# A gate's softplus written with |z| on ScalarE in a hybrid attention and convolution step

## The chip, the cores and the metric

The kernel runs on one core of one Trainium2 chip. The metric is device microseconds (us) of one execution. Beside the times there is one profiled execution, taken by the hardware profiler; its rows are the source of every duration below. The engines are PE (TensorE matmul; PEld its weight loads), DVE (VectorE), ACT (ScalarE), POOL (GpSimd) and SP (SyncE, which issues all DMAs here). The programs are built with a scheduler that fixes each engine's instruction order before the run; on the chip each engine then follows its own list in order and waits on semaphores.

## The reference, cut to what matters

One layer. A normalised input (2048 prompt rows, 16 meta rows, 32 sample rows, 1024 wide) goes through one projection of 4096 columns. Four attention heads and four convolution units of 128 columns each follow, each with a gate z·sigmoid(z) (SiLU); then an output projection, a residual add and a norm.

```
q, k, v, z_a, b_g, c_g, u, z_c = split_proj(rmsnorm(hp, norm_g[l]), w_in[l])
...
o = rmsnorm(o, sub_g) * (1.0 - lam_init)
o = o.reshape(*o.shape[:2], W_ATT) * jax.nn.silu(z_a)
y_c = jax.nn.silu(z_c) * b_g * conv_out
return jnp.concatenate([o, y_c], axis=-1) @ w_o
```

The kernel gets sigmoid(z) as exp(-softplus(-z)), softplus(-z) = log(1 + exp(-z)), since exp and log serve everywhere else in it.

## The kernel before, in words

The prompt is cut into four passes p = 0..3 of 512 rows; pass 0 also carries the 48 meta and sample rows and is projected in two blocks of 272 to 288 columns, the others in one block of 512. In each pass `unit_a(h, p)` projects q, k, v and the gate z of head h, `attend(h, p)` does its two softmaxes and the product with v, and `unit_c(u, p)` does a convolution unit with its own gate. Each projection (`proj`, L225) is 24 matmuls of three split products: weights and inputs are cut into a high and a low part (`wh`, `wl`, `xh`, `xl`), the high ones cast by ACT (L204, L152), the low ones subtracted on POOL or DVE (L78, L153). A projection ends in PSUM (`pj`, two buffers) and is evicted on DVE: q at L254, k at L280, v at L305, z at L352 and L572. The evicted v is transposed by PE (L316), so PE waits there for L305.

Attention scores `s` (L446, L447; three PSUM buffers) are reduced on DVE (L396, or L393 for the last stretch with the bias) and turned to exponentials by ACT (L397), which frees the buffer. `coefs` (L370 to L377) merges the stretches' sums, L400 and L401 scale and combine the two softmaxes, PE transposes the result (L462), ACT and DVE split it (L465, L466) and L469 to L471 multiply it with v.

`softplus_neg(out, z)` (L186 to L191) runs in `ev_z` (L353) and in `ev_g` (L573), once for each block of columns: 40 calls, 24 of them 512 wide (p = 1 to 3) and 16 of them 272 wide (p = 0). `unit_c` follows it with an exponential (L574) and two products; attention keeps it as `l1` until `post`, where L427 adds it to the logarithm of the norm and L428 takes one exponential of the sum.

Ahead of each later pass, `x_stats(p)` squares eight tiles on ACT (L115), reduces them on DVE (L117), `x_rms(p)` builds a diagonal matrix on DVE (L127), multiplies it on PE (L129) and copies it out on ACT (L130); `x_load(p)` splits the new inputs (L152, L153). At the end `out_first` and `out_rest` do the output projection (L693, L685): `load_cat` reads a tile `ct` and splits it (L671, L78), `half_product` adds the residual (L694) and the sum of squares (L695), L727 to L731 scale the rows, and SP stores them (`out<-y`).

Of the kernel before, what the change touches and what calls it, by code (L numbers as in the profile page):

```python
# [13 lines left out]
AF = mybir.ActivationFunctionType  # L14
ALU = mybir.AluOpType
# [32 lines left out]
def hybrid_step(ctx: ExitStack, tc: tile.TileContext, x, xT, ckT, cv, scT, rel_bias, norm_g, w_in,  # L48
# [20 lines left out]
    V, S, G, T = nc.vector, nc.scalar, nc.gpsimd, nc.tensor  # L69
# [3 lines left out]
    def halved(out, a, b, op, engine=None):  # L73

        n = out.shape[-1] if len(out.shape) == 2 else out.shape[1]
        cuts = (0, n // 2, n) if engine is None and n * (out.shape[-1] if len(out.shape) > 2 else 1) > 256 else (0, n)
        for c0, c1 in zip(cuts, cuts[1:]):
            (engine or G).tensor_tensor(out[:, c0:c1], a[:, c0:c1], b[:, c0:c1], op=op)  # L78
# [106 lines left out]

    def softplus_neg(out, z):  # L186

        V.tensor_scalar(out, z, -1.0, 40.0, op0=ALU.mult, op1=ALU.min)
        S.activation(out, out, AF.Exp)
        S.activation(out, out, AF.Ln, bias=1.0)  # L190
        V.scalar_tensor_tensor(out, z, -1.0, out, op0=ALU.mult, op1=ALU.max)  # L191


    pre = {}
# [14 lines left out]
    def proj(col, p, evac):  # L209
        w2 = pre.pop((col, p), None) or w_load(col, p)  # L210
        if p > 0:
            blks = [(0, QT)]
        elif col < CK or CZ <= col < CC or col >= CG:
            blks = [(NM, 288), (288, 560)]
        else:
            blks = [(0, 280), (280, 560)]
        for b0, b1 in blks:
            if p == 0 and col == CV:
                ps = ps_s.tile([P, 512], F32, tag="s", name="pj")[:, :b1 - b0]
            else:  # L220
                ps = ps_j.tile([P, 512], F32, tag="pj", name="pj")[:, :b1 - b0]
            for k in range(KT):
                wh, wl = w2[k // 4]
                for i, (a, b) in enumerate(((wh, xh), (wh, xl), (wl, xh))):
                    T.matmul(ps, lhsT=a[:, k % 4], rhs=b[k][:, b0:b1],  # L225
                             start=(k == 0 and i == 0), stop=(k == KT - 1 and i == 2))
            evac(ps, b0, b1)
# [9 lines left out]
    def unit_a(h, p):  # L237
# [113 lines left out]
        def ev_z(ps, b0, b1):  # L351
            V.tensor_tensor(z32[:, b0:b1], ps, rbs[p][:, b0:b1], op=ALU.mult)  # L352
            softplus_neg(l1[:, b0:b1], z32[:, b0:b1])  # L353
# [63 lines left out]
    def post(n, o32, sq, z, l1, dst):  # L417
        sqh, sql = (ap.tile([P, 2, 256], F32R, tag=t_, name="sqh").rearrange("p a b -> p (a b)")[:, :n]
                    for t_ in ("ah", "al"))
        V.tensor_copy(sqh, sq)  # L420
        V.tensor_tensor(sql, sq, f32(sqh), op=ALU.subtract)
        ps = ps_o.tile([P, 512], F32, tag="po", name="pss")[:, :n]
        T.matmul(ps, lhsT=ones_r, rhs=sqh, start=True, stop=False)
        T.matmul(ps, lhsT=ones_r, rhs=sql, start=False, stop=True)
        f = o_tile(n)
        S.activation(f, ps, AF.Ln, scale=1.0 / P, bias=leps[:, 0:1])
        V.scalar_tensor_tensor(f, f, 0.5, l1, op0=ALU.mult, op1=ALU.add)  # L427
        S.activation(f, f, AF.Exp, scale=-1.0)  # L428
        V.scalar_tensor_tensor(o32, o32, g2[:, 0:1], f, op0=ALU.mult, op1=ALU.mult)
        halved(o32, o32, z, ALU.mult)  # L430
        dma(dst, by_tile(o32) if n == QT else o32)

    def attend(h, p, st):
# [5 lines left out]
        for b in range(2):  # L439
# [40 lines left out]
            S.copy(o32[:, 256 * b:256 * (b + 1)], po)  # L480
            S.activation(sq[:, 256 * b:256 * (b + 1)], po, AF.Square)
        post(QT, o32, sq, z32[:, f0:f0 + QT], l1[:, f0:f0 + QT], cat[p][:, :, h])

    def attend_sample(h, st):
# [37 lines left out]
        V.tensor_tensor(o32[0], o32[0], o32[1], op=ALU.add)  # L522
        S.activation(sq, o32[0], AF.Square)
        post(NS, o32[0], sq, z32[:, NM + QT:], l1[:, NM + QT:], cat_s[:, h])


    def unit_c(u, p):
        tw = NX + QT if p == 0 else QT
        bn = tw + 4 if p == 0 else tw + 2
        ch = g_tile(bn)  # L530
        f0 = NM if p == 0 else 0
        hn = f0 + QT
        V.tensor_copy(ch[:, 0:2], hist[:, u])
        if p == 0:
            V.tensor_copy(ch[:, 2 + hn:4 + hn], scs[:, u])
        c32 = g_tile(tw)

        def ev_c(ps, b0, b1):
            V.tensor_tensor(c32[:, b0:b1], ps, rbs[p][:, b0:b1], op=ALU.mult)
            halved(c32[:, b0:b1], c32[:, b0:b1], rbs[p][:, b0:b1], ALU.mult)  # L540
        proj(CC + u, p, ev_c)

        def spans(b0, b1):
            return [(b0, min(b1, hn), 2)] + ([(hn, b1, 4)] if b1 > hn else [])

        def ev_u(ps, b0, b1):
            for s0, s1, off in spans(b0, b1):
                V.tensor_tensor(ch[:, s0 + off:s1 + off], ps[:, s0 - b0:s1 - b0], c32[:, s0:s1], op=ALU.mult)
        proj(CU + u, p, ev_u)
        V.tensor_copy(hist[:, u], ch[:, hn:hn + 2])  # L550
        if p == 0:
            dma(cT_s[P * u:P * (u + 1)], ch[:, bn - 2:])
        if p == NQ - 1:
            dma(cT_p[P * u:P * (u + 1)], ch[:, bn - 2:])
        yc = g_tile(bn - 2)
        V.tensor_scalar(yc, ch[:, :bn - 2], cw[:, 0, u:u + 1], None, op0=ALU.mult)
        V.scalar_tensor_tensor(yc, ch[:, 1:bn - 1], cw[:, 1, u:u + 1], yc, op0=ALU.mult, op1=ALU.add)
        V.scalar_tensor_tensor(yc, ch[:, 2:], cw[:, 2, u:u + 1], yc, op0=ALU.mult, op1=ALU.add)

        t4 = g_tile(tw)  # L560
        for s0, s1, off in spans(f0, tw):
            halved(yc[:, s0 + off - 2:s1 + off - 2], yc[:, s0 + off - 2:s1 + off - 2], rbs[p][:, s0:s1], ALU.mult)

        def ev_b(ps, b0, b1):
            for s0, s1, off in spans(b0, b1):
                V.tensor_tensor(t4[:, s0:s1], ps[:, s0 - b0:s1 - b0], yc[:, s0 + off - 2:s1 + off - 2], op=ALU.mult)
        proj(CB + u, p, ev_b)
        e, zc = g_tile(tw), g_tile(tw)

        def ev_g(ps, b0, b1):  # L570
            eb = e[:, b0:b1]
            V.tensor_tensor(zc[:, b0:b1], ps, rbs[p][:, b0:b1], op=ALU.mult)  # L572
            softplus_neg(eb, zc[:, b0:b1])  # L573
            S.activation(eb, eb, AF.Exp, scale=-1.0)  # L574
            halved(zc[:, b0:b1], zc[:, b0:b1], t4[:, b0:b1], ALU.mult)
        proj(CG + u, p, ev_g)
        V.tensor_tensor(t4[:, f0:], zc[:, f0:], e[:, f0:], op=ALU.mult)
        dma(cat[p][:, :, 4 + u], by_tile(t4[:, f0:hn]))
        if p == 0:
            dma(cat_s[:, 4 + u], t4[:, hn:])  # L580
# [232 lines left out]
```

## Time and profile before

| what | value |
| --- | --- |
| time, median of 3 runs | 1292.07 us (1292.02 to 1293.26) |
| profiled execution, own time | 1293.26 us |
| its span, first to last instruction | 1291.5 us |
| busy: PE / DVE / ACT / POOL | 1267.5 / 923.9 / 827.5 / 699.0 us |
| mean granted TensorE clock | 0.995 |
| DMA moved | 198.74 MB, mean 154 GB/s |

Busy time is the time in which at least one instruction of the engine runs; matmuls overlap each other, so PE's busy time is not a sum of single durations. The view by stages cuts the span into stretches and gives each engine's busy time in each. The view of waits says which instruction's end ended an idle time. In the timeline a row is start, duration, engine, line, operation, and what is written from what; a bracket gives idle time before the row and what ended it. ACT instructions that stand back to back overlap by a little, so what one costs in a full queue is the distance between starts.

### The profile page before, as it was taken

The page shows a single profiled execution, that of the slowest core. Times are in us where ns is not written, and L with a number is a line of the kernel's source. Part 1 is how long each engine was busy: PE and PEld are TensorE (multiplying, and loading weights), DVE is VectorE, ACT ScalarE, POOL GpSimd, SP SyncE. Part 2 cuts the span into 40 slices and gives each one's busy share as a digit, 9 for nine tenths or more (in the row PEclk, how much of TensorE's full clock was granted, in tenths as well). Part 3 has the DMA queues.
Part 4 walks back from the last instruction along what each step waited for, and adds up shares of the span by engine and source line. Part 5 has one row for each costly group of instructions (what it writes and reads, how often), then busy time and mean ns, then how long its engine had stood idle before and what let it go on. Part 6 is the DMA issues. An engine that isn't in the chain of part 4 may idle for free.

```text
span 1291.5 us, 21630 instructions
## 1 busy us (share of the span) xinstructions
PE 1267.5 (98%) x7058; PEld 1101.4 (85%) x7058; DVE 923.9 (72%) x2086; ACT 827.5 (64%) x2030; POOL 699.0 (54%) x918
## 2 busy tenths in 40 slices
PE   8999999999999998999999999999999999999897
PEld 6999999988888886888888888888888888888675
DVE  8767566567886847787878677767786896856654
ACT  6745454675776647677767567777777786763322
POOL 5775857767565675455556555364656483432200
PEclk9999999999999999999999999999999999999999
DMA  9834444774445347444343453344334543557652
GB/s 290 226 116 129 141 112 116 216 241 149 137 117 159 125 145 228 156 137 134 101 169 124 142 177 114 116 147 119 117 109 141 177 133 124 177 181 237 215 181 81
DMA packets 108048, 198.74 MB, mean 154 GB/s; under 512 B 17408, under 2 KB 45600, under 8 KB 107936
## 3 DMA queue, kind: packets, MB, share of 16 engines
q1 hardware_dynamic: 107936, 197.37, 49.0%
q8 instruction: 55, 0.90, 0.3%
q14 instruction: 57, 0.47, 0.1%
HBM read 145.62 MB, written 43.26 MB: 146 GB/s over the span
## 4 chain that ended last, share of the span: by engine, by line
PE 55%; DVE 3%; DMA 3%; ACT 1%; issue 1%; DVEq 0%; SPq 0%; ACTq 0%
PE pj L225 27%; PE po L693 9%; PE s L446 4%; PE s L447 4%; PE pt L462 3%; PE po L469 2%; PE po L471 2%; PE po L470 2%; DMA out<-y 1%; DMA ct<-cat 1%; PE po L685 1%; DMA y<-y 0%; DVE y L731 0%; PE ptv L316 0%; DVE cs L78 0%
## 5 line engine op out<-in xcount | busy, mean ns | idle before, releaser
L78 POOL TENSOR_TENSOR wl<-wr,wh 128x256 fp32r<-128x256 f32 x480 | 377.4, 810 | 300.6 <-ACT wh L204 279.4
L225 PE MATMUL pj<-xh,wh 128*128 128x512 f32 (+2 forms) x1280 | 456.9, 358 | 3.0 <-DVE g L352 1.3
L225 PE MATMUL pj<-xl,wh 128*128 128x512 f32 (+2 forms) x1280 | 453.6, 355 | 0.9 <-DVE xl L153 0.9
L225 PE MATMUL pj<-xh,wl 128*128 128x512 f32 (+2 forms) x1280 | 452.9, 354 | 0.0
L225 PEld LDWEIGHTS pj<-xh,wh 128*128 128x128 f32 x1280 | 242.5, 190 | 34.8 <-issue 2.3
L225 PEld LDWEIGHTS pj<-xh,wl 128*128 128x128 f32 x1280 | 242.2, 189 | 29.9 <-issue 0.2
L225 PEld LDWEIGHTS pj<-xl,wh 128*128 128x128 f32 x1280 | 242.4, 189 | 29.5 <-DVE xl L153 1.4
L397 ACT ACTIVATE p<-s,nm 128x384 f32<-128x384 f32 (+5 forms) x352 | 208.6, 595 | 68.8 <-DVE nm L396 41.9
L204 ACT CAST wh<-wr 128x512 fp32r<-128x512 f32 x256 | 157.5, 618 | 102.7 <-PE pj L225 72.0
L401 DVE SCALAR_TENSOR_TENSOR p<-p,cf,p 128x384 f32<-128x384 f32 (+5 forms) x176 | 127.1, 751 | 23.9 <-ACT p L400 23.7
L396 DVE TENSOR_REDUCE nm<-s 128x1 f32<-128x384 f32 (+3 forms) x224 | 122.6, 560 | 22.7 <-PE s L447 22.5
L78 POOL TENSOR_TENSOR cll<-ct,chh 128x256 fp32r<-128x256 f32 x80 | 63.1, 815 | 131.2 <-ACT chh L671 131.2
L466 DVE TENSOR_TENSOR al<-pt,ah 128x512 fp32r<-128x512 f32 x144 | 97.2, 684 | 46.7 <-ACT ah L465 46.1
L446 PE MATMUL s<-ks,q 128*128 128x384 f32 (+5 forms) x352 | 127.3, 363 | 1.0 <-ACT p L397 0.8
L447 PE MATMUL s<-ks,q 128*128 128x384 f32 (+5 forms) x352 | 122.5, 349 | 0.0
L400 ACT ACTIVATE p<-p,cf 128x384 f32<-128x384 f32 (+5 forms) x176 | 99.1, 623 | 28.2 <-DVE cf L377 25.3
L465 ACT CAST ah<-pt 128x512 fp32r<-128x512 f32 x144 | 81.2, 585 | 42.7 <-PE pt L462 41.6
L393 DVE CUSTOM_DVE_ANT_0 s<-s,bz 128x512 f32<-128x512 f32 (+5 forms) x128 | 74.7, 588 | 21.5 <-PE s L447 19.0
L462 PE MATMUL pt<-ident,p 128*128 128x128 f32 x544 | 86.0, 272 | 0.0
L470 PE MATMUL po<-al,vh 128*128 128x256 f32 x288 | 82.5, 287 | 0.0
L469 PE MATMUL po<-ah,vh 128*128 128x256 f32 x288 | 81.7, 284 | 0.0
L471 PE MATMUL po<-ah,vl 128*128 128x256 f32 x288 | 81.2, 282 | 0.0
(237 smaller groups left out, 2192.2 us busy)
## 6 DMA issues: line engine op xcount, KB each, us to landing
wr<-in_w_in SPq DMA_DIRECT2D x128, 512.0 KB, 3.7
ct<-cat SPq DMA_DIRECT2D x28, 512.0 KB, 4.7
q<-q SPq DMA_DIRECT2D x64, 128.0 KB, 2.9
out<-y SPq DMA_DIRECT2D x32, 256.0 KB, 3.6
ks<-ksd SPq DMA_DIRECT2D x8, 776.0 KB, 5.3
xr<-in_x SPq DMA_DIRECT2D x24, 256.0 KB, 4.9
out<-g SPq DMA_DIRECT2D x24, 256.0 KB, 3.3
xt<-in_xT SPq DMA_DIRECT2D x24, 256.0 KB, 4.9
```

What stands on the lines that cost most here:

```text
L78: (engine or G).tensor_tensor(out[:, c0:c1], a[:, c0:c1], b[:, c0:c1], op=op)
L204: S.copy(wh, wi)
L225: T.matmul(ps, lhsT=a[:, k % 4], rhs=b[k][:, b0:b1], start=(k == 0 and i == 0), stop=(k == KT - 1 and i == 2))
L396: V.tensor_reduce(nm[:, c, j:j + 1], s, op=ALU.min, axis=AX.X)
L397: S.activation(pr[j][c], s, AF.Exp, bias=nm[:, c, j:j + 1], scale=-1.0, accum_out=l[:, c, j:j + 1])
L401: V.scalar_tensor_tensor(a0, a1, cf[:, 1, j:j + 1], a0, op0=ALU.mult, op1=ALU.add)
L446: T.matmul(ps, lhsT=qd[c][0][:, qs], rhs=ks[c][:, col:col + w], start=True, stop=False)
L447: T.matmul(ps, lhsT=qd[c][1][:, qs], rhs=ks[c][:, col:col + w], start=False, stop=True)
L462: T.transpose(pt[:, i, P * qi:P * (qi + 1)], cols(aa[qi], NM + P * (2 * j + i), P), ident)
L469: T.matmul(po, lhsT=vh[:, kt], rhs=ah[:, i], start=(kt == 0), stop=False)
L470: T.matmul(po, lhsT=vh[:, kt], rhs=al[:, i], start=False, stop=False)
L693: T.matmul(ps, lhsT=a[k][:, :rows], rhs=b[k], start=(k == 0 and i == 0), stop=(k == KT - 1 and i == 2))
```

## The change

`softplus_neg` gets log(1 + exp(-|z|)) from three ACT instructions, absolute value, exponential and logarithm, and then min(z, 0) minus that on DVE. What comes out is -softplus(-z) and no longer softplus(-z), so its two readers change a sign: L427 subtracts where it added, and L574 loses its factor of -1. The first DVE instruction, -z clamped at 40 (L188), is gone; exp(-|z|) cannot overflow.

```
     def softplus_neg(out, z):
-        V.tensor_scalar(out, z, -1.0, 40.0, op0=ALU.mult, op1=ALU.min)
-        S.activation(out, out, AF.Exp)
+        S.activation(out, z, AF.Abs)
+        S.activation(out, out, AF.Exp, scale=-1.0)
         S.activation(out, out, AF.Ln, bias=1.0)
-        V.scalar_tensor_tensor(out, z, -1.0, out, op0=ALU.mult, op1=ALU.max)
+        V.scalar_tensor_tensor(out, z, 0.0, out, op0=ALU.min, op1=ALU.subtract)
...
         S.activation(f, ps, AF.Ln, scale=1.0 / P, bias=leps[:, 0:1])
-        V.scalar_tensor_tensor(f, f, 0.5, l1, op0=ALU.mult, op1=ALU.add)
+        V.scalar_tensor_tensor(f, f, 0.5, l1, op0=ALU.mult, op1=ALU.subtract)
         S.activation(f, f, AF.Exp, scale=-1.0)
...
             softplus_neg(eb, zc[:, b0:b1])
-            S.activation(eb, eb, AF.Exp, scale=-1.0)
+            S.activation(eb, eb, AF.Exp)
```

The line numbers stay. L188 is a DVE instruction before and an ACT instruction after.

The scheduler places all engines' work anew, so the lists differ in many places. PE keeps its 7058 matmuls. Three places matter below.

The first is ACT's list at the start of pass 2, where it squares the tiles for pass 3 (L115) and copies out `rb` (L130); `p_6563` is an exponential of pass 1's last attention. The rows with + are new in the list, those with - have left that place.

```order
 L115 ACTIVATE xr,ssq<-xr 128x512 x2
 L130 COPY rb<-pb 128x512
+L188 ACTIVATE g<-g 128x512
+L115 ACTIVATE xr,ssq<-xr 128x512
 L397 ACTIVATE p_6563,l<-s,nm 128x384
-L115 ACTIVATE xr,ssq<-xr 128x512 x2
+L115 ACTIVATE xr,ssq<-xr 128x512
```

The absolute value of the gate comes ahead of that exponential, and one of the squares moves ahead of it too.

The second is DVE's list some 17 us later, up to the eviction of v (L305), for which PE's transposes wait. Before (L393 stands as two `ISA` rows, a reduction and the reading of its result):

```order
L375 RECIPROCAL r_6616<-M_6617 128x2
L184 TENSOR_TENSOR x_8734<-x_8734,x_8735 128x4
L376 TENSOR_TENSOR r_6616<-r_6616,lam_141 128x2
L127 TENSOR_TENSOR dg<-ident,x_8734 128x512
L377 TENSOR_TENSOR cf<-nm,r_6616 128x2x2
L393 ISA s,nm<-s,bz 128x512
L393 ISA nm 128x1
L305 TENSOR_TENSOR g<-pj,rb 128x512
```

And in the changed program:

```order
L127 TENSOR_TENSOR dg<-ident,x_8734 128x512
L375 RECIPROCAL r_6616<-M_6617 128x2
L396 TENSOR_REDUCE nm<-s 128x1
L393 ISA s,nm<-s,bz 128x512
L393 ISA nm 128x1
L376 TENSOR_TENSOR r_6616<-r_6616,lam_141 128x2
L305 TENSOR_TENSOR g<-pj,rb 128x512
```

L377 has moved behind the eviction; L396, which stood ahead of L181 before, now stands behind L127.

The third is PE's list in the last stage, where the last attention's closing product (L479) stands between matmuls of the output projection.

```order
 L693 MATMUL po<-wq_14519,chh 128x512
 L693 MATMUL po<-ks_14517,chh 128x512
+L479 MATMUL po<-am_117,ms_121 128x256
 L693 MATMUL po<-ks_14517,cll 128x512
 L693 MATMUL po<-wq_14520,chh 128x512
 L693 MATMUL po<-ks_14517,chh 128x512
-L479 MATMUL po<-am_117,ms_121 128x256
 L693 MATMUL po<-ks_14517,cll 128x512
```

It has moved ahead by three of them.

## The prediction

> **What bounds the kernel now.** I read the page first: busy time by engine, then the chain that ended last.
>
> ```profile
> PE 1267.5 (98%) x7058; PEld 1101.4 (85%) x7058; DVE 923.9 (72%) x2086; ACT 827.5 (64%) x2030; POOL 699.0 (54%) x918
> ...
> PE 55%; DVE 3%; DMA 3%; ACT 1%; issue 1%; DVEq 0%; SPq 0%; ACTq 0%
> ```
>
> PE is idle for 1291.5 - 1267.5 = 24.0 us. The chain names no other engine with more than 3%. Where the 24 us lie is in the view by stages (stretch, length, busy time of PE, PEld, DVE, ACT, POOL, granted clock, DMA share, GB/s).
>
> ```profile
> 0.00:90.00 90.00, 83.19 (x566) 76.53 (x567) 66.23 (x165) 55.42 (x136) 59.60 (x89) 1.00 0.72 212
> ...
> 262.00:480.00 218.00, 218.00 (x1117) 184.60 (x1117) 156.81 (x364) 140.70 (x345) 139.45 (x179) 1.00 0.48 149
> 480.00:520.00 40.00, 34.82 (x148) 27.71 (x148) 29.68 (x70) 30.08 (x77) 23.35 (x27) 0.91 0.77 243
> 520.00:755.00 235.00, 234.75 (x1259) 203.27 (x1258) 176.72 (x382) 162.81 (x387) 130.11 (x168) 1.00 0.43 136
> ...
> 770.00:1048.00 278.00, 277.93 (x1480) 239.75 (x1479) 217.57 (x455) 205.49 (x489) 153.07 (x193) 1.00 0.41 128
> ...
> 1160.00:1228.00 68.00, 64.33 (x288) 51.87 (x287) 43.30 (x101) 24.95 (x66) 15.59 (x22) 0.97 0.69 221
> 1228.00:1291.50 63.50, 55.89 (x242) 43.36 (x240) 32.91 (x87) 17.19 (x52) 3.00 (x4) 0.97 0.40 131
> ```
>
> PE's idle time lies in four places: 6.8 us in the first 90, 5.2 us from 480 to 520, 3.7 us from 1160 to 1228, 7.6 us at the end. In the long stretches between (262 to 480, 520 to 755, 770 to 1048) it is 0.3 us in 731. So an instruction taken off DVE or put on ACT gives or costs time only if it moves one of these places or makes a new one. Who ended PE's waits:
>
> ```profile
> PE pv L601 <- DMA oh<-in_ohd: 4.1, 1, 4.1
> PE ptv L316 <- DVE g L305: 3.4, 2, 3.2
> PE po L693 <- ACT cs L671: 3.2, 2, 2.0
> PE pj L225 <- DVE g L352: 1.3, 2, 1.1
> ...
> PE s L446 <- ACT p L397: 0.8, 1, 0.8
> ```
>
> No row is an instruction of the softplus (L188 to L191) or one that reads it (L427, L574, L577). The gate's chain ends in buffers that PE reads much later, as `cat` of the output projection. When the calls run:
>
> ```profile
> L188 DVE TENSOR_SCALAR g<-g x40: 292/480/957, 41.0 to 1048.1; 128x512 f32<-128x512 f32 x24, 128x272 f32<-128x272 f32 x16
> ```
>
> The first starts at 41.0 us, behind the start's wait for a DMA, and the last at 1048.1, before the last stage.
>
> **The change part by part.** The durations, by shape (line, engine, operation, count, then busy us, mean ns, and idle time before):
>
> ```profile
> L191 DVE SCALAR_TENSOR_TENSOR g<-g 128x512 f32<-128x512 f32 x24 | 18.5, 770 | 6.7 <-ACT g L190 6.7
> ...
> L189 ACT ACTIVATE g<-g 128x512 f32<-128x512 f32 x24 | 15.1, 630 | 7.9 <-DVE g L188 7.7
> L188 DVE TENSOR_SCALAR g<-g 128x512 f32<-128x512 f32 x24 | 14.7, 613 | 0.5
> L427 DVE SCALAR_TENSOR_TENSOR o<-o,g 128x512 f32<-128x512 f32 x16 | 13.1, 817 | 4.3 <-ACT o L426 4.2
> ...
> L189 ACT ACTIVATE g<-g 128x272 f32<-128x272 f32 x16 | 6.9, 429 | 11.0 <-DVE g L188 10.9
> ...
> L188 DVE TENSOR_SCALAR g<-g 128x272 f32<-128x272 f32 x16 | 6.6, 412 | 0.4
> ```
>
> Removed from DVE: 24 x 613 + 16 x 412 ns = 21.3 us. Added to ACT: 40 absolute values. The trace has none, so I bound one by its neighbour L189, an activation of the same tile: above by its mean (630 and 429 ns), below by the 0.52 us between its start and the next in a full queue (499.47 to 499.99 below). I take the mean: 24 x 630 + 16 x 429 ns = 22.0 us. DVE falls to about 903 us, ACT rises to about 849 us, both under PE's 1267.5. The kept DVE instruction swaps multiply and maximum for minimum and subtract on the same two tiles, and L427 and L574 swap a sign; no row prices the new operations. The rows for other pairs of operations on two such tiles are L427 (817 ns) and L191 (770 ns), 47 ns apart; over the 60 instructions whose operations change (40 of L191, 20 of L427) that is 2.8 us of DVE time either way, and I take 0 between. All of this is hidden by PE's own work, which fills 99.9% of the long stretches; without that cover the change would cost the 0.7 us by which ACT gains more than DVE loses.
>
> The Trainium skill speaks against this move: "ScalarE: Activation LUTs", section "Rules for kernel authors", sends minimum, multiply and the like to VectorE and keeps ScalarE for transcendentals. By that rule the move would make the busier queue of the two ACT's, and the time would be that of the rival below in which ACT is late; by the rows the two engines' mean price differs by 17 ns a call and ACT keeps more idle time than DVE, which is the forecast's side.
>
> What is left are the places where PE does wait. **First place, 480 to 520.** DVE's and ACT's rows there, then PE's:
>
> ```profile
> 493.01 0.41 DVE L188 TENSOR_SCALAR g<-g 128x512 f32<-128x512 f32 x1
> ...
> 496.63 0.17 DVE L371 TENSOR_TENSOR nm<-nm,M 128x4 f32<-128x4 f32 x1 [2.32 <-ACT p L397]
> ...
> 502.59 0.16 DVE L117 TENSOR_REDUCE x<-ssq 128x4 f32<-128x8 f32 x1 [0.39 <-ACT xr L115]
> ...
> 513.00 0.68 DVE L377 TENSOR_TENSOR cf<-nm,r 128x4 f32<-128x4 f32 x1
> 513.60 0.69 DVE L393 CUSTOM_DVE_ANT_0 s<-s,bz 128x512 f32<-128x512 f32 x1
> ...
> 514.21 0.68 DVE L305 TENSOR_TENSOR g<-pj,rb 128x512 f32<-128x512 f32 x1
> ```
>
> ```profile
> 499.47 0.63 ACT L189 ACTIVATE g<-g 128x512 f32<-128x512 f32 x1
> 499.99 0.62 ACT L204 CAST wh<-wr 128x512 fp32r<-128x512 f32 x1
> ...
> 501.83 0.63 ACT L115 ACTIVATE xr<-xr 128x512 f32<-128x512 f32 x1
> ```
>
> ```profile
> 511.26 0.39 PE L446 MATMUL s<-ks,q 128*128 128x272 f32 x1 [0.78 <-ACT p L397]
> ...
> 514.95 1.11 PE L316 MATMUL ptv<-ident,g 128*128 128x128 f32 x4 [3.17 <-DVE g L305]
> ...
> 516.29 0.63 PE L225 MATMUL pj<-xl,wh 128*128 128x512 f32 x1
> ...
> 519.66 0.39 PE L225 MATMUL pj<-xh,wh 128*128 128x512 f32 x1
> ```
>
> The removed instruction (493.01) stands ahead of a DVE wait of 2.32 us for ACT, so taking it away there buys nothing. From L117 (502.59), which waits for ACT's last square, to L305 (514.21) DVE runs without a break: 11.6 us. In the new lists ACT has the absolute value ahead of its squares (+0.52 us on L117), and DVE has L377 behind L305 (-0.60, from 513.00 to 513.60). L396 moves behind L127, so PE's wait of 0.78 us for the score buffer grows by what the wait of 3.17 us for L305 shrinks; together they stay near 4 us. Sum: 0.52 - 0.60 = -0.1; I take 0, with bounds of -0.6 and +1.1 us (only the one, or the absolute value and the moved square both ahead). After the idle time the clock is lower: from 516.29 to 519.66 eight matmuls start 0.42 us apart, against 0.23 us in the row of L693 below, and the granted clock of the stretch is 0.91. With the idle time unchanged this stays too.
>
> **Second place, 1160 to 1228.** The chain of waits there:
>
> ```profile
> 1209.07 4.06 DMA out<-y
> ...
> 1213.93 4.72 DMA ct<-cat
> ...
> 1226.53 27.76 PE po L693 x119
> ```
>
> The waits are those of stores, loads and casts that follow each other through SP. The softplus has no part in it. What the new order does: L479 stands three L693 matmuls earlier, 3 x 27.76/119 = 0.7 us, so PE has 0.7 us less of attention to fill the chain with and 0.7 us more behind it: sum 0. SP's list has one read of `ct` two stores earlier and is else alike; I take 0, with one link of the chain, 4.7 us, as the bound either way.
>
> Sum against the profile's own 1293.26 us: 0 at both places. The median of the runs shown is 1.2 us below that execution; the change keeps the distance. **Forecast: 1292.1 us, no change**, with its own range of 1290 to 1294.
>
> **The rivals.**
>
> *Faster: the relief breaks the first stall.* If DVE's 11.6 us run shortens by as little as a few contended instructions, PE's idle time there falls, and below some length the clock no longer drops. All 5.2 us of idle time plus eight matmuls at 0.19 us too much (1.5 us) is the bound: 6.7 us. Half the idle time and the whole clock loss, 2.6 + 1.5 = 4.1, gives 1288.0. For it: DVE is busy for the whole run. Against it: its start hangs on ACT, which got more.
>
> *Slower: ACT is late with exponentials.* The score buffers are three, and the exponential that frees one stands in ACT's queue; an absolute value ahead of it delays it by 0.52 us. This decides only where PE already stands at the fourth score. ACT is fullest from 770 to 1048 (205.49 of 278 us, 74%). If half of the 16 wide calls of passes 2 and 3 hit such a place, that is 8 x 0.52 = 4.2 us: 1296.3. Against it: in the whole run PE waited for L397 once, 0.8 us.
>
> *The output chain shifts by a link.* 4.7 us either way: 1287.4 or 1296.8. Nothing of the change is in it, but the order ahead of it is new.
>
> *The absolute value is not in the loaded table.* ACT would change tables twice a call. The new list holds one table load only, as now. Its row:
>
> ```profile
> 0.73 1.28 ACT L70 ACT_TABLE_LOAD   x1 [0.73 <-PEq L798]
> ```
>
> 80 x 1.28 = 102 us on ACT would still fit below PE but would hold up scores and weights; with a tenth of it reaching PE, 1302. The Trainium skill, "ScalarE: Activation LUTs", section "Table sets: the hidden batching unit", says that the cheap functions, the absolute value among them, are in every set; the list agrees with that.
>
> **How the numbers follow.** Forecast 0.48; faster by the first stall 0.22; ACT late 0.18; the chain later 0.07, earlier 0.04; the table 0.01. A measurement of this kernel tells about 0.2% (2.6 us) from no change. That makes faster 0.26, same 0.48, slower 0.26. The range for 8 in 10 reaches past both rivals' middle values by about 1 us: 1287 to 1297.
>
> **What would show it.** Right: DVE near 903 and ACT near 849 us busy, PE's busy time and its idle share in the long stretches as now, L316 still waiting for L305 behind L127 with the wait for L397 grown, and the granted clock still near 0.91 there. Wrong: PE waits for L397 in many places (ACT late), or a stretch from 480 to 520 without idle time (faster), or a wait on L671 in the last stage that has doubled or gone.

## The result: 0.2 to 0.4 per cent slower

| kernel | median of runs | ratio to the kernel before, 95% interval |
| --- | --- | --- |
| before (5 runs) | 1292.42 us (1292.02 to 1293.89) | 1 |
| changed (5 runs, same chip) | 1298.56 us (1296.02 to 1300.23) | 1.0038 [1.0027, 1.0050] |
| changed, on another chip (12 runs; before there 1293.21) | 1296.76 us (1293.09 to 1298.87) | 1.0024 [1.0014, 1.0034] |

The forecast was 1292.1 us and no change. The first measurement lies above the range of 1287 to 1297, the second at its upper end; both intervals lie above 1. The changed kernel's own runs spread by 4 us, and the time follows the granted clock: 1296.02 us at a mean clock of 0.996, which is the execution profiled below, and 1300.23 at 0.993. So the two profiles are 1296.02 - 1293.26 = 2.8 us apart, where the medians of that chip are 6.1 apart; what is read from the profiles below is the smaller difference.

The page of the changed kernel, first row, and its view of PE's waits (us in all, times, longest):

```profile
PE 1268.4 (98%) x7058; PEld 1099.9 (85%) x7058; DVE 905.7 (70%) x2046; ACT 844.9 (65%) x2070; POOL 696.8 (54%) x918
...
PE s L446 <- ACT p L397: 5.3, 3, 4.1
...
PE ptv L316 <- DVE g L305: 0.5, 2, 0.3
```

PE's own busy time has hardly moved (1267.5 before), DVE's fell by 18.2 us and ACT's rose by 17.4. The wait of L316 for L305 has gone from 3.4 us to 0.5, and the wait of L446 for L397 has grown from 0.8 to 5.3. The view by stages for the changed kernel stands second. The stretch 840 to 1060 of pass 3 is not in the prediction, so its row of the kernel before comes first:

```profile
840.00:1060.00 220.00, 220.00 (x1177) 189.92 (x1177) 174.38 (x353) 164.64 (x394) 129.12 (x156) 1.00 0.43 134
```

```profile
262.00:480.00 218.00, 217.47 (x1110) 182.90 (x1109) 153.75 (x359) 144.18 (x352) 138.71 (x178) 1.00 0.48 149
480.00:520.00 40.00, 34.58 (x151) 27.91 (x150) 29.57 (x65) 30.72 (x78) 24.37 (x29) 0.96 0.73 232
...
770.00:1048.00 278.00, 276.43 (x1478) 237.84 (x1477) 215.05 (x457) 209.75 (x503) 144.61 (x187) 1.00 0.42 123
...
840.00:1060.00 220.00, 218.52 (x1174) 187.88 (x1173) 171.62 (x355) 169.33 (x405) 117.24 (x149) 1.00 0.43 129
...
1160.00:1228.00 68.00, 64.62 (x303) 52.52 (x302) 43.80 (x97) 25.41 (x67) 17.62 (x24) 1.00 0.71 224
```

The place on which the prediction spent most words, 480 to 520, has 5.4 us without PE against 5.2 before, at a granted clock of 0.96 against 0.91. What is new is idle time inside the long stretches: 0.5 us up to 480 and 1.6 us in pass 3, where there was 0.3 in all.

Idle time shows only part of such a loss: matmuls of 0.39 us start 0.23 us apart here, so one that starts a tenth of a microsecond late still overlaps its neighbour. A finer measure is used below as *late starts*: for each pair of successive matmuls of the trace, how far the distance between their starts exceeds what is usual behind a matmul of the first one's shape in the kernel before (its 30th percentile; a shorter distance counts against it), summed over a stretch. It counts matmuls at the low clock too, and a slight usual scatter everywhere. All kernels issue the same matmuls, so over the whole span the sums differ by what PE's work takes longer from its first start to its last.

| late starts, us | 200 to 350 | 350 to 480 | 480 to 530 | 850 to 1060 | whole span |
| --- | --- | --- | --- | --- | --- |
| before | 4.4 | 1.8 | 9.1 | 2.8 | 48.7 |
| changed | 5.6 | 2.0 | 8.4 | 5.8 | 51.5 |
| changed, second profile (e14) | 5.7 | 2.0 | 10.4 | 5.5 | 52.2 |

Pass 3 gained 3 us of late starts and 200 to 350 1.2 us; the other stretches together lost 1.4, which makes the 2.8 us between the two profiles. That is where the profile says the time went; the runs had to tell why.

### The profile page after: what moved, and what is told of

The parts are those of the page before. It is cut to its first block, busy times and chain, and to the rows that moved or that the text cites. A ratio compares the mean times of both kernels' runs of the same rounds, so it can differ in the third digit from the quotient of the medians.

```text
span 1294.2 us, 21636 instructions
## 1 busy us (share of the span) xinstructions
PE 1268.4 (98%) x7058; PEld 1099.9 (85%) x7058; DVE 905.7 (70%) x2046; ACT 844.9 (65%) x2070; POOL 696.8 (54%) x918
## 4 chain that ended last, share of the span: by engine, by line
PE 56%; DVE 2%; ACT 2%; DMA 2%; issue 0%; SPq 0%; DVEq 0%; ACTq 0%
PE pj L225 26%; PE po L693 12%; PE s L446 4%; PE s L447 4%; PE pt L462 4%; PE po L470 2%; PE po L471 2%; PE po L469 2%; DMA ct<-cat 1%; DMA out<-y 1%; PE po L685 1%; DMA xr<-in_x 0%; ACT p L397 0%; PE ptv L316 0%; ACT xr L115 0%
## 5 line engine op out<-in xcount | busy, mean ns | idle before, releaser
L78 POOL TENSOR_TENSOR wl<-wr,wh 128x256 fp32r<-128x256 f32 x480 | 377.9, 810 | 313.3 <-ACT wh L204 277.4
L225 PE MATMUL pj<-xh,wh 128*128 128x512 f32 (+2 forms) x1280 | 455.0, 357 | 2.8 <-DVE g L352 1.0
L225 PE MATMUL pj<-xl,wh 128*128 128x512 f32 (+2 forms) x1280 | 454.2, 355 | 1.1 <-DVE xl L153 1.1
L225 PE MATMUL pj<-xh,wl 128*128 128x512 f32 (+2 forms) x1280 | 452.7, 354 | 0.0
L225 PEld LDWEIGHTS pj<-xh,wh 128*128 128x128 f32 x1280 | 242.2, 189 | 32.7 <-ACT bvec L603 1.7
L225 PEld LDWEIGHTS pj<-xl,wh 128*128 128x128 f32 x1280 | 242.1, 189 | 32.5 <-issue 2.4
L225 PEld LDWEIGHTS pj<-xh,wl 128*128 128x128 f32 x1280 | 241.8, 189 | 30.4 <-issue 1.1
L397 ACT ACTIVATE p<-s,nm 128x384 f32<-128x384 f32 (+5 forms) x352 | 208.1, 594 | 69.0 <-DVE nm L396 36.4
L396 DVE TENSOR_REDUCE nm<-s 128x1 f32<-128x384 f32 (+3 forms) x224 | 123.0, 560 | 25.0 <-PE s L447 24.2
L401 DVE SCALAR_TENSOR_TENSOR p<-p,cf,p 128x384 f32<-128x384 f32 (+5 forms) x176 | 126.1, 745 | 18.8 <-ACT p L400 18.5
L446 PE MATMUL s<-ks,q 128*128 128x384 f32 (+5 forms) x352 | 127.9, 365 | 5.6 <-ACT p L397 5.3
L78 POOL TENSOR_TENSOR cll<-ct,chh 128x256 fp32r<-128x256 f32 x80 | 62.0, 800 | 120.3 <-ACT chh L671 120.3
L447 PE MATMUL s<-ks,q 128*128 128x384 f32 (+5 forms) x352 | 122.5, 349 | 0.0
L400 ACT ACTIVATE p<-p,cf 128x384 f32<-128x384 f32 (+5 forms) x176 | 98.8, 621 | 24.9 <-DVE cf L377 24.5
L393 DVE CUSTOM_DVE_ANT_0 s<-s,bz 128x512 f32<-128x512 f32 (+5 forms) x128 | 74.3, 590 | 30.6 <-PE s L447 22.8
L462 PE MATMUL pt<-ident,p 128*128 128x128 f32 x544 | 84.5, 273 | 0.2 <-DVE p L401 0.2
L471 PE MATMUL po<-ah,vl 128*128 128x256 f32 x288 | 81.2, 282 | 0.0
```

Source lines behind the costliest of these rows:

```text
L225: T.matmul(ps, lhsT=a[:, k % 4], rhs=b[k][:, b0:b1], start=(k == 0 and i == 0), stop=(k == KT - 1 and i == 2))
L396: V.tensor_reduce(nm[:, c, j:j + 1], s, op=ALU.min, axis=AX.X)
L397: S.activation(pr[j][c], s, AF.Exp, bias=nm[:, c, j:j + 1], scale=-1.0, accum_out=l[:, c, j:j + 1])
L401: V.scalar_tensor_tensor(a0, a1, cf[:, 1, j:j + 1], a0, op0=ALU.mult, op1=ALU.add)
L446: T.matmul(ps, lhsT=qd[c][0][:, qs], rhs=ks[c][:, col:col + w], start=True, stop=False)
L447: T.matmul(ps, lhsT=qd[c][1][:, qs], rhs=ks[c][:, col:col + w], start=False, stop=True)
```

## The experiments

Two causes are mixed in the changed kernel. The work moves from DVE to ACT, and the scheduler, which works from its own costs, writes new lists for all engines: of PE's 7019 instructions in the lists 3924 stand at another position than before, of the 1918 that DVE keeps 1081. To part the two, kernels got an order by hand: a step behind the whole program adds edges, for order alone, between successive instructions of each engine out of a table. Such edges cost nothing by themselves: e9 and e10 below have them on nearly the old order and take 0.9995 and 1.0001 of the time before.

```
         hybrid_step(tc, *args)
+        pin(tc)
...
+def pin(tc):
...
+    for seq in seqs:
...
+            if prev is not None:
+                tc.add_manual_dep(traced[at], traced[prev].name, info(), reason="pinned order")
```

### e1 and e2: the work without the order, the order without the work

e1 has the new gates in the lists of the kernel before, each absolute value right ahead of its exponential. e2 has the old gates in the changed kernel's lists, each clamp in DVE's list right behind the eviction of its z.

> The changed gates in the order of before: every engine's list is that of the kernel before, with the 40 absolute values on ACT right ahead of their exponentials and without the 40 clamps on DVE. If the new order of the lists is what costs (order theory), this runs like before: 1292, between 1290 and 1294 us, with DVE near 903 and ACT near 849 us busy, and PE's idle time from 480 to 520 as 1.0 and 3.2 us in two pieces. If the 22 us more on ACT are what costs (ACT theory), it stays near 1298 (1296 to 1300) and PE waits for exponentials (L397) in several places.

> The gates of before in the order of the changed kernel: every engine's list is that of the changed kernel, with the 40 clamps back on DVE, each right behind the eviction of its z, and without the 40 absolute values on ACT. Order theory: 1297 to 1300 us, as the changed kernel, with one idle piece of PE of about 4.4 us near 511. ACT theory: 1291 to 1293 us.

Measured: e1 1294.35 us (11 runs), ratio 1.0007 [0.9999, 1.0016]; e2 1298.13 us (5 runs), ratio 1.0031 [1.0019, 1.0043]. The order alone, with not one instruction of the change in it, costs about what the change costs. The work alone costs little or nothing by e1: its interval reaches just below 1. PE's waits in e1, then in e2:

```profile
PE ptv L316 <- DVE g L305: 3.6, 2, 3.2
PE s L446 <- ACT p L397: 1.2, 1, 1.2
...
PE s L446 <- POOL ks L78: 0.5, 1, 0.5
```

```profile
PE s L446 <- ACT p L397: 4.7, 3, 3.6
```

e1 waits as the kernel before does, with 0.4 us more for L397 and 0.3 more for the split keys (0.2 before). e2 shows the changed kernel's long wait for L397, though no absolute value stands on its ACT.

### e3 and e4: the evictions of the first attention of pass 2 first

The long wait of e2 and of the changed kernel lies at the start of pass 2. e3 is the changed kernel with four DVE rows (L396, L393 with its read, L305) moved ahead of the root of the next normalization (L181 to L127). e4 does the same to the kernel before (there L396 stood ahead already).

```
 L78 TENSOR_TENSOR wl<-wr,wh 128x512
+L396 TENSOR_REDUCE nm<-s 128x1
+L393 ISA s,nm<-s,bz 128x512
+L393 ISA nm 128x1
+L305 TENSOR_TENSOR g<-pj,rb 128x512
 L181 TENSOR_TENSOR x_8735<-x_8734 128x4
...
 L127 TENSOR_TENSOR dg<-ident,x_8734 128x512
...
-L396 TENSOR_REDUCE nm<-s 128x1
-L393 ISA s,nm<-s,bz 128x512
-L393 ISA nm 128x1
...
-L305 TENSOR_TENSOR g<-pj,rb 128x512
```

> The changed kernel in its own order with one local move on DVE: at the start of pass 2 the reduction of a score tile (L396), one with bias (L393) and the eviction of v (L305) stand ahead of the six small steps for the next pass's norm (L181 to L184, L127) instead of behind them. If the one idle piece of 4.4 us at 511, and the lower clock behind it, is the loss, the piece shrinks to under 1.2 us and the time falls by 3 to 6 us, to 1292 to 1295.5 us, with less spread between runs. If the loss is spread over many places, the time falls by under 2 us.

> The kernel before in its own order with the same local move (L393 and L305 ahead of L181 to L184 and L127; L396 stands there already). PE's two idle pieces there (0.8 and 3.2 us) shrink to under 1 us together, and with them the two windows of half clock that followed: 1286 to 1289.5 us. If that idle time comes back at the next wait, 1291 to 1293 us.

Measured: e3 1293.5 us (12 runs), ratio 1.0002 [0.9992, 1.0011]; e4 1289.88 us (5 runs), ratio 0.9969 [0.9957, 0.9981]. The stretch in e3, then in e4:

```profile
480.00:520.00 40.00, 36.56 (x159) 29.40 (x158) 29.49 (x65) 30.02 (x76) 24.54 (x29) 0.96 0.75 229
```

```profile
480.00:520.00 40.00, 37.61 (x173) 30.09 (x172) 29.51 (x69) 30.57 (x78) 23.78 (x28) 1.00 0.76 236
```

Against their own starting points PE is busy 2.0 and 2.8 us longer there, and in e4 the clock is not lowered. For a moment this looked like the explanation: the changed kernel joins two pieces of idle time (0.78 and 3.17 us) into one of 4.1, e3 shortens it to 2.1 and is level with the kernel before. But the same move gains e4 about as much. It repairs something that both kernels have, and e3 and e4 stay 0.33% apart, as far as the changed kernel and the kernel before. e9 puts that to the test.

### e9: the new order of that place alone

The kernel before, old gates, its own lists, save for the 13 DVE instructions at the start of pass 2, which stand as in the changed program: L396 behind L127, L393 and L305 behind it, L377 last.

```
 L78 TENSOR_TENSOR wl<-wr,wh 128x512
-L396 TENSOR_REDUCE nm<-s 128x1
 L181 TENSOR_TENSOR x_8735<-x_8734 128x4
...
+L127 TENSOR_TENSOR dg<-ident,x_8734 128x512
 L375 RECIPROCAL r_6616<-M_6617 128x2
+L396 TENSOR_REDUCE nm<-s 128x1
+L393 ISA s,nm<-s,bz 128x512
+L393 ISA nm 128x1
 L376 TENSOR_TENSOR r_6616<-r_6616,lam_141 128x2
-L127 TENSOR_TENSOR dg<-ident,x_8734 128x512
+L305 TENSOR_TENSOR g<-pj,rb 128x512
 L377 TENSOR_TENSOR cf<-nm,r_6616 128x2x2
-L393 ISA s,nm<-s,bz 128x512
-L393 ISA nm 128x1
-L305 TENSOR_TENSOR g<-pj,rb 128x512
```

> The kernel before with old gates and its own lists, save for 13 DVE instructions at the start of pass 2, which stand as the changed program has them: L396 behind L127, L393 and L305 behind it, L377 behind L305. The prediction's step: PE's wait for the score grows by what the wait for L305 shrinks, together they stay, so no change: ratio 0.9995 to 1.0005, PE's idle time from 505 to 520 at 4.5 to 5 us. Rival (this order of 13 instructions is what costs the changed kernel its 0.4%): ratio 1.002 to 1.004, idle time there at 6 us or more. If neither local order nor the work's move costs that much, the 0.3% of the new lists lies elsewhere in them.

Measured: 1292.58 us (12 runs), ratio 0.9995 [0.9986, 1.0003]. PE's row at that place and the stretch in e9, then the row in the changed kernel:

```profile
514.72 0.59 PE L446 MATMUL s<-ks,q 128*128 128x272 f32 x1 [3.93 <-ACT p L397]
```

```profile
480.00:520.00 40.00, 34.42 (x150) 27.42 (x149) 29.84 (x68) 30.37 (x78) 22.88 (x27) 0.96 0.77 238
```

```profile
515.94 0.60 PE L446 MATMUL s<-ks,q 128*128 128x272 f32 x1 [4.11 <-ACT p L397]
```

So e9 has the changed kernel's joined wait and the clock of its profile, 0.96, and loses nothing. The prediction's step for this place holds, and the reading of e3 as the cause falls.

### e12, e13 and e14: which half of the new lists

Left are the lists elsewhere. e12 is the changed kernel with its own lists up to about 765 us, the start of pass 3, and the lists of e1 from there; e13 is the reverse; e14 is the changed kernel itself, on the same chip. For each engine the lists were joined at a point at which both have issued the same instructions. What differs is the table of `pin`; in outline (the kernel holds the finished table), for e12:

```
-table[engine] = changed[engine]
+table[engine] = changed[engine][:cut[engine]] + e1[engine][cut[engine]:]
```

> The changed kernel, whose lists are its own up to about 765 us (start of pass 3) and from there the lists of e1, that is those of the kernel before. In the traces so far the matmuls of the long stretch from 850 to 1060 start 3.2 us late in sum in every kernel with the new lists (14.1 to 14.4 us over their usual spacing) and never with the old ones (10.9 to 11.2). If that is the new lists' main cost: the sum there falls back to 11, and the time is 3 us less than that of the changed kernel on this chip, ratio to before 1.0005 to 1.0025. If the cost comes of the start of pass 2 or of the granted clock alone: as the changed kernel, ratio 1.003 to 1.005.

> The reverse: the lists of e1 up to about 765 us and from there those of the changed kernel. If the late starts of 850 to 1060 come of the lists there: sum of 14 in that stretch and about 3 us over e1, ratio 1.002 to 1.004; 200 to 350 and 480 to 530 as in e1. If they come of what stands ahead: as e1, ratio 1.000 to 1.0015.

> The changed kernel as it is, on the same chip as the two runs before it, since its own time was taken on another chip than that of e1 to e11. Its loss by the runs so far: 0.3% for the lists (e2) and 0.1 to 0.2% for the absolute values on ACT (e1, e5, e11): ratio 1.003 to 1.005.

Measured, ratios to the kernel before: e12 1.0014 [1.0005, 1.0023], e13 1.0026 [1.0016, 1.0036], e14 1.0024 [1.0014, 1.0034]. With the lists from pass 3 on taken back, the median falls by 1.2 us (1296.76 to 1295.56), which is not clear of noise: the intervals of e12 and e14 overlap. With those lists alone put in, e13 costs as much as the changed kernel, and 0.19% more than e1, which is clear of noise. The views of pass 3, e12, e13 and e14:

```profile
840.00:1060.00 220.00, 220.00 (x1177) 189.97 (x1176) 168.81 (x348) 167.34 (x398) 127.74 (x157) 1.00 0.44 134
```

```profile
840.00:1060.00 220.00, 218.54 (x1175) 188.25 (x1174) 170.73 (x355) 169.31 (x404) 115.59 (x148) 1.00 0.43 129
```

```profile
840.00:1060.00 220.00, 218.48 (x1176) 188.19 (x1174) 171.59 (x356) 169.30 (x404) 115.86 (x147) 1.00 0.44 129
```

| late starts, us | 200 to 350 | 350 to 480 | 480 to 530 | 850 to 1060 |
| --- | --- | --- | --- | --- |
| e1 (old lists) | 4.4 | 2.2 | 9.9 | 2.8 |
| e12 (new, then old) | 5.7 | 2.0 | 8.5 | 2.8 |
| e13 (old, then new) | 4.7 | 2.2 | 10.0 | 5.4 |
| e2 (new lists, old gates) | 6.1 | 2.0 | 9.1 | 5.6 |

(The expectation of e12 gives larger sums, by another count of the usual distances; the difference of 3 us is the same.) Each half brings its own late starts along, whatever stands in the other. e3 and e4, 0.33% or 4.3 us apart by time, fit too: 5.8 against 2.8 us in the stretch of pass 3, 5.7 against 4.4 from 200 to 350 (over the whole span their profiles differ by 3.2 us). Two places make nearly all of the 3 us of pass 3, one near 855 us (L462 for L401, L316 for L305) with 1.1 us and one near 1009 with 1.6, in every profile with the new lists there. The second in the timeline of PE, changed and then before:

```profile
1007.77 0.40 PE L225 MATMUL pj<-xh,wl 128*128 128x512 f32 x1
...
1009.07 0.27 PE L462 MATMUL pt<-ident,p 128*128 128x128 f32 x1
1010.28 0.50 PE L446 MATMUL s<-ks,q 128*128 128x512 f32 x1 [0.93 <-ACT p L397]
```

```profile
1006.76 0.82 PE L462 MATMUL pt<-ident,p 128*128 128x128 f32 x6
...
1008.35 0.39 PE L225 MATMUL pj<-xh,wl 128*128 128x512 f32 x1
...
1009.73 0.39 PE L225 MATMUL pj<-xh,wl 128*128 128x512 f32 x1
```

Before, seven projection matmuls stand together in PE's list at 1008.35 to 1009.73 between two scores, while ACT and DVE work on the first. In the changed list one stands there, at 1007.77; more have been spent earlier. The view by stretches for L225 alone (PE's busy time and starts, then PEld's), before and then changed:

```profile
990.00:1003.00 13.00, 6.00 (x23) 4.11 (x24) 1.00 0.36 105
1003.00:1014.00 11.00, 6.66 (x26) 4.54 (x25) 1.00 0.47 164
```

```profile
990.00:1003.00 13.00, 8.33 (x34) 5.89 (x33) 1.00 0.40 122
1003.00:1014.00 11.00, 4.25 (x17) 2.88 (x17) 1.00 0.34 108
```

Before, 23 and 26 matmuls; now 34 and 17. The work is the same, and more of it stands where little was late. That this is why PE waits at 1009 is read from the lists and not shown by a run.

### e7: the wait at 1009 attacked on ACT

e3 with one more move: two of the exponentials go ahead of the four scalings (L400) behind which they stand at 1007.

```
+L397 ACTIVATE p_12549,l<-s,nm 128x400
+L397 ACTIVATE p_12550,l<-s,nm 128x400
 L400 ACTIVATE p_12365<-p_12365,cf 128x400
 L400 ACTIVATE p_12377<-p_12377,cf 128x512
 L400 ACTIVATE p_12389<-p_12389,cf 128x384
 L400 ACTIVATE p_12401<-p_12401,cf 128x512
-L397 ACTIVATE p_12549,l<-s,nm 128x400
-L397 ACTIVATE p_12550,l<-s,nm 128x400
```

> The changed kernel with the local move of e3 and one more: on ACT two L397 go ahead of the four L400 behind which they stood at 1007, where PE waits 1.2 us. If the rest of the loss lies in such single places: 1.0 to 1.2 us less than e3, ratio 0.999 to 0.9997, the idle piece at 1008 gone. If the wait only goes to another place (L401 and the transposes then come later): as e3, ratio 1.000 to 1.0005, with a new wait within a few us of 1010.

Measured: 1293.1 us (11 runs), ratio 0.9998 [0.9989, 1.0007], the same as e3 within the intervals. PE's wait at the place is as long (its late starts there stay at 1.6 us more than before) and now is one for DVE:

```profile
PE pt L462 <- DVE p L401: 1.0, 1, 1.0
```

So it is not that exponential's place in ACT's queue that costs there: put first, it delays the scalings and the transposes behind them by the same amount. That fits the missing filler on PE; a kernel with only PE's matmuls moved back was not tried.

### e5, e11 and e6: the price of the absolute values themselves

e5 is e4 with the new gates, e11 is e8 (below) with the new gates, as e1 is the kernel before with them. e6 is e1 with a second absolute value of the first's result, which changes no number.

```
         S.activation(out, z, AF.Abs)
+        S.activation(out, out, AF.Abs)
         S.activation(out, out, AF.Exp, scale=-1.0)
```

> The lists of the kernel before with the local move of e4 (L393 and L305 ahead of L181 at the start of pass 2), and the new gates in them: the 40 absolute values right ahead of their exponentials on ACT, the 40 clamps gone from DVE. Order theory: the move of the work between the engines costs what it cost in e1 (0.9 us, near the resolution), so e4's 1289.9 plus 0 to 1 us: 1290 to 1291, ratio 0.997 to 0.9985. Rival (the absolute values use up the room that the local move opened): ratio 0.9995 to 1.0005, with PE's wait at 512 back at 2 us or more.

> The new gates in the lists of e8, as e5 is to e4: a third measure of what the absolute values on ACT cost by themselves. They cost 0.9 us in e1 and 1.5 in e5 (with the distance of before's medians taken off, 1.8). If that is a real price of about 1.2 us: 1288.5 to 1290, ratio 0.9968 to 0.998. If it was chance: as e8, ratio 0.996 to 0.9968.

> The kernel of e1 with every absolute value taken twice (the second of a value that is already not negative), so ACT has another 40 activations, some 21 us, in the lists of the kernel before. Theory that ACT's extra work is hidden: as e1, ratio 1.000 to 1.002, ACT near 867 us busy, PE's wait for L397 near 1.2 us. Rival (ACT is late with exponentials, each absolute value ahead of one costs 0.5 us in some eight places): the dose doubles, another 2 to 4 us over e1, ratio 1.002 to 1.004, with PE's wait for L397 at 3 us or more in several places.

Measured: e5 1291.41 us, ratio 0.9987 [0.9978, 0.9996], that is 0.18% over e4; e11 1290.95 us, ratio 0.9984 [0.9975, 0.9992], 0.20% over e8; e6 1300.17 us, ratio 1.0050 [1.0036, 1.0064], 0.43% over e1. With e1's 0.07% the first 40 absolute values cost 0.9 to 2.6 us, and the next 40 some 5.6. The price is real, then (e5 and e11 are clear of noise against e4 and e8, e1 is not clear of 1), and it grows faster than the load. Where the first are paid, by PE's waits of e5 (0.8 and 0.2 us for the same rows without them):

```profile
PE s L446 <- ACT p L397: 1.4, 1, 1.4
...
PE s L446 <- POOL ks L78: 0.5, 1, 0.5
```

And the second, in e6 (its lines behind L188 count one higher, so L398 is the exponential, L467 the split of the weights, L447 and L471 the matmuls that wait):

```profile
PE po L471 <- DVE al L467: 1.8, 1, 1.8
PE s L447 <- ACT p L398: 1.8, 2, 1.7
...
PE s L447 <- POOL ks L78: 1.1, 1, 1.1
```

The same two waits grow again, and a third opens at 395 us (late starts of 350 to 480: 5.9 us against 2.2 in e1): there ACT's scalings (L401 in its count) are late, DVE waits for them before it can split the weights, and PE waits for DVE. DVE's row and PE's:

```profile
393.45 3.06 DVE L402 SCALAR_TENSOR_TENSOR p<-p,cf,p 128x272 f32<-128x272 f32 x3 [1.43 <-ACT p L401]
```

```profile
397.16 0.39 PE L471 MATMUL po<-al,vh 128*128 128x256 f32 x1 [1.83 <-DVE al L467]
```

Behind this wait the granted clock is low, in the two stretches of 2 us from 398 on:

```profile
398.00:400.00 2.00, 2.00 (x12) 2.00 (x11) 1.50 (x5) 1.94 (x6) 1.33 (x2) 0.50 0.03 12
400.00:402.00 2.00, 2.00 (x9) 1.71 (x8) 0.88 (x2) 2.00 (x7) 0.09 (x1) 0.65 0.34 78
```

That is 3.4 us at half clock, 1.7 us lost, in a place where e1 has a clock of 1.00. So nearly half of the 3.7 us at this place, and with it part of why the second 40 cost more, is one wait that has grown long enough to lower the clock.

Between 850 and 1060, where ACT is as full as anywhere, e6 has 3.1 us against 2.8: next to nothing. By this it is not the busy share that decides, but whether PE stands close behind ACT.

### e10: the new formula on VectorE

In the lists of the kernel before, -|z| as min(z, -z) by one DVE instruction in the clamp's place, and the rest as changed.

```
-        S.activation(out, z, AF.Abs)
-        S.activation(out, out, AF.Exp, scale=-1.0)
+        V.scalar_tensor_tensor(out, z, -1.0, z, op0=ALU.mult, op1=ALU.min)
+        S.activation(out, out, AF.Exp)
```

> The new formula without the move to ACT: -|z| is made on DVE as the smaller of z and -z, by one instruction of L191's form in the clamp's place (770 ns in place of 613 for the wide tile), the rest as in the changed kernel, in the lists of the kernel before. DVE gains 24 x 157 + 16 x about 100 ns = 5.4 us, and 60 instructions have other operations. Theory that both are hidden: ratio 0.9995 to 1.0007, DVE near 929 us busy. Rival (DVE's work is not hidden either, or the swapped operations cost up to 47 ns each): ratio 1.001 to 1.003.

Measured: 1292.91 us (11 runs), ratio 1.0001 [0.9992, 1.0009]. By the groups of its profile:

```profile
L188 DVE SCALAR_TENSOR_TENSOR g<-g 128x512 f32<-128x512 f32 x24 | 21.0, 876 | 0.5
```

DVE gives 263 ns more for each wide tile than the clamp did (613), is busy for 932.0 us in place of 923.9, and it costs nothing that can be measured. DVE's time was hidden here and ACT's was not.

### e8: a version that beats both

Old gates, e4's lists, and two more moves on DVE: L352 ahead of two of the five L153 near 490 us, and L396 and L393 ahead of the L78 at 509.

```
+L352 TENSOR_TENSOR g<-pj,rb 128x512
 L153 SCALAR_TENSOR_TENSOR xl_6525<-xt,ng,xh_6524 128x512
 L153 SCALAR_TENSOR_TENSOR xl_6531<-xt,ng,xh_6530 128x512
-L352 TENSOR_TENSOR g<-pj,rb 128x512
...
+L396 TENSOR_REDUCE nm<-s 128x1
+L393 ISA s,nm<-s,bz 128x512
+L393 ISA nm 128x1
 L78 TENSOR_TENSOR wl<-wr,wh 128x512
-L396 TENSOR_REDUCE nm<-s 128x1
-L393 ISA s,nm<-s,bz 128x512
-L393 ISA nm 128x1
```

> The kernel before with e4's local move and two more on DVE: L352 ahead of two of the five L153 (at 486 to 491, where PE waits 1.35 us for L352), and L396 and L393 ahead of the L78 at 509.4 (where PE waits 0.8 us for L397). If PE's waits are those of single late instructions: both idle pieces shrink, together 1.5 to 2 us off e4's 1289.9: 1288 to 1288.5, ratio 0.9955 to 0.9965. If what is moved behind is late next (xl at 492, wl at 512): as e4, ratio 0.997 to 0.998, with PE waiting for L153 or L78 in its place.

Measured: 1287.66 us (5 runs, 1287.53 to 1289.64), ratio 0.9964 [0.9951, 0.9976]: 4.7 us under the kernel before, though not clearly under e4 (0.9969). PE's waits:

```profile
PE pj L225 <- ACT rb L130: 1.3, 1, 1.3
PE pj L225 <- DVE xl L153: 1.2, 3, 0.5
PE s L446 <- ACT p L397: 0.8, 1, 0.8
```

The wait for L352 (1.2 us in e4) is down to 0.2, and one of 1.3 us for L130 has come 4 us later; the wait for L397 did not move. So it is e4's move that carries the gain; the two others are not shown to add to it. With the new gates on top (e11) it is 1290.95 us, still under the kernel before.

## Why the prediction was wrong

**Engine loads: right.** DVE 905.7 us for about 903, ACT 844.9 for about 849. An absolute value took 632 and 428 ns, against 630 and 429 taken from its neighbour:

```profile
L188 ACT ACTIVATE g<-g 128x512 f32<-128x512 f32 x24 | 15.2, 632 | 4.2 <-DVE g L572 3.2 <-DVE g L352 1.0
...
L427 DVE SCALAR_TENSOR_TENSOR o<-o,g 128x512 f32<-128x512 f32 x16 | 12.4, 775 | 1.0 <-ACT o L426 1.0
```

**Swapped operations: right.** L191 stayed at 770 ns for the wide tile, L427 went from 817 to 775; e10 costs nothing.

**First place, 480 to 520: right in its sum.** "PE's wait of 0.78 for the score buffer grows by what the wait of 3.17 for L305 shrinks; together they stay near 4 us": they are 4.1 and 0.5 us in the changed kernel, 3.93 in e9, and e9's ratio is 0.9995. "With the idle time unchanged this stays too" can't be told from one profile. The clock is 0.96 there, not 0.91, but it differs between executions with the same waits (last section): over 480 to 530 it is 0.93 before and in e14, the changed kernel again, and 0.97 in the changed profile and in e10, which has the old waits. The absolute value's own delay, put at 0.52 us and set against L377's 0.60, is real without that offset: 0.4 us more for L397 in e1 and 0.3 for the keys.

**The step that failed: "in the long stretches between (262 to 480, 520 to 755, 770 to 1048) it is 0.3 us in 731. So an instruction taken off DVE or put on ACT gives or costs time only if it moves one of these places or makes a new one."** The sentence names the possibility of a new place, and the sum then gives it nothing: the stretches were taken as covered by PE's own work, and the new order was looked at in two places. It had changed more than half of PE's list. That a stretch is full in the old order says that its filler stood in the right places, not that it is full in any order. The new lists cost 0.31% without the work (e2), and those from pass 3 on alone 0.19% (e13 less e1) or 0.10% (e14 less e12, not clear of noise). The two new places at 855 and 1009 us, 2.7 us of late starts together, lie in a stretch that the prediction counted as full.

**"Without that cover the change would cost the 0.7 us by which ACT gains more than DVE loses": wrong.** DVE's time and ACT's are not worth the same here: 8 us more on DVE cost nothing (e10), 17 us on ACT 0.9 to 2.6 us.

**The rival "ACT is late with exponentials"**, at 1296.3 us, came near the time and saw the right row, L446 waiting for L397. (The chain that shifts by a link, 1296.8, came nearer by number alone: PE waits 2.9 us for L671, 3.2 before.) As a mechanism it is the smaller part: not eight places of 0.52 us in passes 2 and 3, but 0.4 to 0.6 us in one place and 0.3 at another. The 5.3 us of that row in the changed kernel are a matter of order, and mostly not a loss.

The prediction weighed a rule of the Trainium skill, "ScalarE: Activation LUTs", section "Rules for kernel authors", that minimum, multiply and the like belong on VectorE. The runs agree with it: e5 and e11 pay for the absolute value on ScalarE, and e10, which does it on VectorE, does not. What the prediction made of the rule, that ACT would become the busier queue of the two, did not come: ACT is busy for 844.9 us, DVE for 905.7, and ACT's work costs time all the same.

**Second place and the end: right within a microsecond.** PE is busy 64.62 us from 1160 to 1228, against 64.33.

**The table: right.** The changed profile has one load, as before, and an absolute value costs what the exponential behind it does (632 ns both).

**"The change keeps the distance" between profile and median: wrong.** It was 1.2 us before; here the profiled execution lies 2.5 us below the median. The changed kernel's runs have granted clocks of 0.993 to 0.996, and its profile caught the highest.

What stays open: the parts do not add up better than to about 0.1%. On the chip of e12 to e14, the changed kernel's 0.24% would be 0.07 to 0.20% for the absolute values and 0.10 to 0.19% for the lists from pass 3 on; the first half's lists are then worth between nothing and 0.07% (e14 against e13, e12 against e1), though 1.2 us of late starts are seen there. Why the first chip gave 0.38% is not settled; the intervals overlap.

## What to carry to other kernels

Where a scheduler orders the program, a change of one instruction's engine or cost is also a change of order everywhere. Price the two apart: pin the old order and put the new work into it, pin the new order and leave the old work in. And a busy bottleneck engine in the old order is cover for the work of the others only as long as its filler stands where the others are late; compare its whole list, above all in the stretches that look full, before taking them at nothing.

## What the runs showed of the hardware

An idle piece of PE shorter than the two of the kernel before together can already lower the granted clock. PE's row behind the idle piece at the start of pass 2, in e3 and in e5, each with the stretches of 2 us behind it:

```profile
514.01 0.39 PE L446 MATMUL s<-ks,q 128*128 128x272 f32 x1 [2.12 <-ACT p L397]
```

```profile
514.00:516.00 2.00, 1.99 (x9) 1.80 (x10) 1.97 (x6) 0.62 (x2) 1.92 (x4) 0.65 0.93 277
516.00:518.00 2.00, 2.00 (x7) 1.52 (x6) 1.97 (x8) 0.28 (x1) 1.69 (x2) 0.50 1.02 373
518.00:520.00 2.00, 2.00 (x10) 1.64 (x9) 1.24 (x5) 2.00 (x6) 0.00 (x0) 1.00 1.05 393
```

```profile
512.87 0.40 PE L446 MATMUL s<-ks,q 128*128 128x272 f32 x1 [1.44 <-ACT p L397]
```

```profile
514.00:516.00 2.00, 2.00 (x11) 1.61 (x10) 2.00 (x7) 0.00 (x0) 1.59 (x3) 1.00 0.89 278
516.00:518.00 2.00, 2.00 (x10) 1.63 (x9) 1.30 (x4) 1.68 (x4) 0.00 (x0) 1.00 0.99 334
```

Behind 2.12 us of idle time the clock is at half for some 3.4 us, beginning about 0.6 us after PE is at work again; in 4 us that is 16 matmuls in place of 21. Behind 1.44 us it stays at 1.00. At this place it also stays at 1.00 in e4, e8 and e11 (0.85, 0.77 and 1.45 us) and falls in e7 (1.87 us), as it does behind the 1.83 us at 397 in e6. A clock of 0.91 over 40 us is 3.6 us lost, part of it while PE stood still; 0.96 is 1.6.

How long the clock stays low is not settled by the idle time. The kernel before waits 0.78 and 3.17 us here and has a clock of 0.93 from 480 to 530; e10 waits 0.77 and 3.18 us. The changed kernel waits 4.11 us and has 0.97; e14, the same program, waits 4.54 us. Their rows, e10 and then e14:

```profile
480.00:530.00 50.00, 44.77 (x206) 36.29 (x205) 36.48 (x82) 36.90 (x92) 28.44 (x34) 0.97 0.69 221
```

```profile
480.00:530.00 50.00, 44.12 (x192) 35.62 (x191) 35.50 (x79) 36.55 (x92) 27.42 (x33) 0.93 0.67 211
```

And in the last stage of e5 a longer wait has no low clock behind it at all:

```profile
1223.42 0.50 PE L693 MATMUL po<-ks,cs 128*128 128x512 f32 x1 [3.08 <-ACT cs L671]
```

```profile
1224.00:1226.00 2.00, 1.86 (x8) 1.55 (x9) 1.86 (x7) 0.08 (x1) 0.00 (x0) 1.00 0.44 156
```

So in these traces an idle piece of PE costs its length up to about 1.4 us, and from about 1.8 us on it can cost some 1.6 us more for each slow stretch of 3.4 us that it brings, which is none, one or two. That is why three DVE rows, moved, gain e4 4 us: it has 4.8 us of late starts from 480 to 530, against 9.1 before.

The Trainium skill, "TensorE: Matmul & The Clock Gate", section "Why this matters for your kernels", advises against idle gaps of PE over about 3 us, and Part 1 of that page has the clock judged in free-running windows of 3413 ns. The length of the slow stretch agrees with the window; the gap does not: 2.12 us was enough here, and 3.08 us in e5 was not.
